# Bias products of the up projection on 32 rows of TensorE, and a new row order in the chunks of w_down

## The chip, the cores and the metric

The kernel runs on one core of a Trainium2 chip. The metric is the device time of one execution in microseconds (us), lower is better. Time before the change: 1526.08 us, the median of three runs (1525.84 to 1527.07).

## The reference

One block of an encoder on 512 frames of width 1024, in float32: a layer norm, a mixer (latent attention with 8 heads and an HGRN2 recurrence with 4 heads, which share one input projection and one output projection `w_o`), a residual with a layer norm, a mixture of 32 experts of which each frame takes four, and a residual with a layer norm. Each expert computes

```
hb  = xb @ w_up[e] + b_up[e]              # 128 slots, 1024 -> 2048
glu, lin = split(hb)                      # 1024 each
act = min(glu, 7) * sigmoid(1.702 * glu) * (clip(lin, -7, 7) + 1)
y   = act @ w_down[e] + b_down[e]         # 1024 -> 1024
```

`b_up` is a table of 32 rows (one for each expert) of 2048 values. The change touches how `b_up[e]` gets into the up projection, how the rows of `w_down[e]` lie in SBUF, and nothing else of the mathematics.

## The kernel before

**Precision.** Every large product is made of three: a float32 value is split into a high part that TensorE takes at its full rate, and the rest, and `mm3` (L408 to L411) adds high times high, high times low and low times high in PSUM.

**The stream of weights.** `Stream` (class at L43) loads w_o in 4 chunks and then, for each expert, w_up in 8 chunks and w_down in 4, each of 1 MB as 128x2048. SP issues the loads (L74) as soon as a raw buffer is free. ACT makes the high part (`w_hi_t`, L87) and DVE the low part (`w_lo_t`, L89); with the low part a raw buffer is free again. Four high and four low buffers stand between the split and TensorE.

**One expert.** `up_begin` (L416) takes four PSUM banks, one for each 512 of the 2048 columns, and puts the bias there first: four bf16 products `bias_mm` (L413 and L414) whose stationary operand is a column of the selector `erow_b`, spread over 128 columns, and whose moving operand is 512 columns of `bias`. `bias` holds the 32 rows of b_up as high, middle and low bf16 parts on partitions 0 to 31, 32 to 63 and 64 to 95, and zeros on the last 32; the selector has a one on the three rows of the expert. Then come 8 chunks of w_up with 12 products each; ACT and DVE make the activation; `act_T` (L446) transposes its 128x512 halves in 128x128 pieces (L451); and 4 chunks of w_down follow, 12 products each, in two banks. Chunk k of w_down holds rows 256k to 256k+255, row p and row 128+p on partition p (`dn_src`, L214), so transposed piece i of the activation is columns 128i to 128i+127. Experts follow one another without a gap, the transposes and routing products of the next expert (L368, small bf16 products on 32 of the columns of TensorE) between the chunks. This stage is in an order written out by hand.

**The mixer.** `run_mixer` is ordered by a scheduler: the program is written as generators that are woven together, and the scheduler then puts each engine's instructions in one order from its own estimates. At the end of the mixer TensorE has the last projections (L938 to L940 with `mw_hi`), whose results ACT and DVE take as `gs` (L1542, L1543); the levels of the recurrence (L1260 and L1271 on TensorE, with a masked copy `hsc`, L1261 and L1273, and a product `QF`, L1283, on DVE between two levels); and the first half of the output projection, `out_part` (L1588), eight groups of 12 products of `w_o` with `cat`. `cat` is the normed attention: `attn_out` makes its high part on ACT (L1408) and its low part on DVE (L1409), four pieces each.

**Preparing the bias.** `prepare_up` (L321, called at L1567, ahead of the loads of the residual rows at L1578 in the program) runs beside the last projections: four loads of b_up (L328) and twelve moves into `bias` (L335) on ACT's queue, three copies of 128x512 on ACT (L331) and two subtractions of 128x512 on DVE (L333). The selector is made once at the start of the program (L147 to L154).

Of the kernel before, what the change touches and what calls it, by code (L numbers as in the profile page):

```python
# [120 lines left out]
class Consts:  # L121
    def __init__(self, nc, pool, tmp):
# [25 lines left out]
        t = tmp.tile([128, NE], F32, name="sel_t")  # L148
        nc.vector.tensor_scalar(self.erow, jp[:, :NE], 0.0, None, op0=ALU.is_equal)
        for r in (1, 2):  # L150
            nc.vector.tensor_scalar(t, jp[:, :NE], -float(r * NE), None, op0=ALU.is_equal)
            nc.vector.tensor_add(self.erow, self.erow, t)
        self.erow_b = pool.tile([128, NE], BF, name="erow_b")
        nc.vector.tensor_copy(self.erow_b, self.erow)  # L154


class Moe:
# [55 lines left out]
    @staticmethod  # L213
    def dn_src(w, k):  # L214
        return [(lambda t: t.rearrange("p (k n) -> p k n", k=2),
                 w[256 * k:256 * (k + 1), :].rearrange("(k p) n -> p k n", p=128))]
# [104 lines left out]
    def prepare_up(self, tmp):  # L321

        nc = self.nc
        nc.gpsimd.memset(self.bias[96:128], 0.0)

        bq = tmp.tile([128, 512], F32, name="prep_b")
        for q in range(4):
            nc.scalar.dma_start(bq[32 * q:32 * q + 32], self.a["b_up"][0][:, 512 * q:512 * q + 512])  # L328
        for r in range(3):
            pt = tmp.tile([128, 512], BF, name=f"prep_p{r}")  # L330
            nc.scalar.copy(pt, bq)  # L331
            if r < 2:
                nc.vector.tensor_sub(bq, bq, pt)  # L333
            for q in range(4):
                nc.scalar.dma_start(self.bias[32 * r:32 * r + 32, 512 * q:512 * q + 512],  # L335
                                    pt[32 * q:32 * q + 32, :])
# [76 lines left out]
    def bias_mm(self, ps, sel, j):  # L413
        self.nc.tensor.matmul(ps, sel, self.bias[:, 512 * j:512 * j + 512], start=True, stop=False)  # L414

    def up_begin(self, sel):  # L416
        ps = [self.ps_up.tile([128, 512], F32, name="ps_up_t") for _ in range(4)]
        for j in range(4):
            self.bias_mm(ps[j], sel, j)
# [26 lines left out]
    def act_T(self, h):  # L446

        nc, ah, al = self.nc, self.ah, self.al
        p = self.ps_tr.tile([128, 4, 128], F32, name="ps_tr", tag="tr")
        for i in range(4):  # L450
            nc.tensor.transpose(p[:, i, :], self.l_bufs[h][:, 128 * i:128 * i + 128], self.c.ident)  # L451
# [122 lines left out]
    def sel_of(self, e):  # L574
        return self.c.erow_b[:, e:e + 1].to_broadcast([128, 128])
# [107 lines left out]
    def overflow(self, out):  # L683
# [3 lines left out]
        with tc.For_i(0, n, 1) as i:  # L687
# [28 lines left out]
            sc = self.xp.tile([128, 1], F32, name="ov_sc")  # L716
# [1017 lines left out]
```

## Time and profile before

| what | value |
|---|---|
| median of 3 runs | 1526.08 us (1525.84 to 1527.07) |
| profiled execution | 1526.0 us |
| its span | 1524.2 us |
| mean granted clock of TensorE | 0.986 of full speed |
| TensorE busy (PE) | 1463.3 us, 96% of the span |
| VectorE busy (DVE) | 1325.1 us, 87% |
| ScalarE busy (ACT) | 1074.7 us, 71% |
| GpSimd busy (POOL) | 263.8 us, 17% |

The profiled execution is 0.08 us under the median and inside the range of the three runs, so its rows may stand for them. The span is 1.8 us shorter than its own time; that rest lies around the span. In all that follows, times are microseconds from the start of the span, and PE is TensorE's products, PEld its loads of the stationary operand. The experts take the stretch from 338 us to about 1495 us; what lies ahead is the layer norm, the mixer and the routing, what lies behind is the last layer norm.

### The profile page before, as it was taken

Reading aid. Unit: us, or ns where it says so; the run is one execution under the profiler, and the core shown is the slowest. Engines: PE = TensorE matmul, PEld = TensorE weight load, DVE = VectorE, ACT = ScalarE, POOL = GpSimd, SP = SyncE. Lnnn points to the kernel's source line nnn. Section 1 sums busy time; section 2 is a strip of 40 time slices with the busy share of each in tenths; the row PEclk is TensorE's granted clock in tenths of the full one; section 3 lists DMA queues with packets and bytes.
Section 4 is the critical chain, followed back from the end, with each engine's and each line's share of the span. In section 5 each row is a group of like instructions: output and inputs, shape, how many; then the busy total and the mean of one; then the engine's idle time right before and its main releaser. Section 6 shows DMA issues by size and latency. Waiting matters only on the chain. (4 is left out here: it accounts for less than half of the span.)

```text
span 1524.2 us, 20021 instructions
## 1 busy us (share of the span) xinstructions
PE 1463.3 (96%) x7366; PEld 1208.1 (79%) x7398; DVE 1325.1 (87%) x1519; ACT 1074.7 (71%) x1149; POOL 263.8 (17%) x249
## 2 busy tenths in 40 slices
PE   7999999979999999999999999999999999999983
PEld 5878998767888888888888888888888888888863
DVE  8867877668999999999999999999999999999975
ACT  4678453347777777777777777777777777777762
POOL 5120414230111111111111111111111111111033
PEclk9999999999999999999999999999999999999997
DMA  5222145367999999999999999999999999999943
GB/s 201 86 81 56 29 147 189 145 212 288 346 366 371 374 358 374 369 377 364 366 376 356 375 361 372 359 378 371 374 359 371 374 368 370 372 366 365 362 152 119
DMA packets 100730, 457.15 MB, mean 300 GB/s; under 512 B 14032, under 2 KB 24697, under 8 KB 67859
## 3 DMA queue, kind: packets, MB, share of 16 engines
q1 hardware_dynamic: 86002, 425.51, 74.4%
q0 software_dynamic: 12672, 29.50, 6.6%
q8 instruction: 60, 0.98, 0.3%
q10 hardware_dynamic: 1952, 0.80, 0.2%
q14 instruction: 44, 0.35, 0.1%
HBM read 447.26 MB, written 24.64 MB: 310 GB/s over the span
## 5 line engine op out<-in xcount | busy, mean ns | idle before, releaser
L89 DVE TENSOR_TENSOR w_lo_t<-w_raw,w_hi_t 128x2048 fp32r<-128x2048 f32 (+1 forms) x391 | 881.3, 2274 | 87.5 <-ACT w_hi_t L87 86.8
L87 ACT CAST w_hi_t<-w_raw 128x2048 fp32r<-128x2048 f32 (+1 forms) x391 | 724.8, 1900 | 1.7 <-PE ps_up_t L411 1.2
L409 PE MATMUL ps_up_t<-w_hi_t,xh 128*128 128x512 f32 x1024 | 420.0, 410 | 0.0
L411 PE MATMUL ps_up_t<-w_hi_t,xl 128*128 128x512 f32 x1024 | 403.4, 394 | 0.0
L410 PE MATMUL ps_up_t<-w_lo_t,xh 128*128 128x512 f32 x1024 | 400.2, 391 | 0.0
L473 POOL DMA_INDIRECT acc_dram<-h,idx x31 | 97.4, 3142 | 955.1 <-ACT h L472 748.4
L411 PEld LDWEIGHTS ps_up_t<-w_hi_t,xl 128*128 128x128 f32 x1024 | 192.7, 188 | 43.6
L409 PEld LDWEIGHTS ps_up_t<-w_hi_t,xh 128*128 128x128 f32 x1024 | 193.2, 189 | 39.7 <-issue 0.8
L410 PEld LDWEIGHTS ps_up_t<-w_lo_t,xh 128*128 128x128 f32 x1024 | 193.4, 189 | 37.4
L411 PE MATMUL ps_dn_t<-w_hi_t,h 128*128 128x512 f32 x512 | 199.8, 390 | 1.1 <-DVE h L455 1.1
L409 PE MATMUL ps_dn_t<-w_hi_t,h 128*128 128x512 f32 x512 | 200.1, 391 | 0.3 <-ACT h L454 0.3
L410 PE MATMUL ps_dn_t<-w_lo_t,h 128*128 128x512 f32 x512 | 199.9, 390 | 0.0
L411 PEld LDWEIGHTS ps_dn_t<-w_hi_t,h 128*128 128x128 f32 x512 | 96.5, 189 | 21.6 <-DVE h L455 1.5
L409 PEld LDWEIGHTS ps_dn_t<-w_hi_t,h 128*128 128x128 f32 x512 | 96.6, 189 | 20.5 <-ACT h L454 0.5
L410 PEld LDWEIGHTS ps_dn_t<-w_lo_t,h 128*128 128x128 f32 x512 | 96.5, 189 | 20.1
L403 ACT CAST xh<-ps_tr 128x512 fp32r<-128x512 f32 x64 | 37.6, 588 | 88.6 <-PE ps_tr L400 88.6
L454 ACT CAST h<-ps_tr 128x512 fp32r<-128x512 f32 x64 | 37.5, 588 | 79.4 <-PE ps_tr L451 79.4
L472 ACT ACTIVATE h<-ps_dn_t,gate_s 128x512 f32<-128x512 f32 x62 | 42.4, 689 | 65.0 <-PE ps_dn_t L411 65.0
L938 PE MATMUL pj<-mw_hi,hT 128*128 128x256 f32 (+1 forms) x192 | 60.2, 314 | 2.8 <-ACT hT L1059 1.7
L939 PE MATMUL pj<-mw_lo,hT 128*128 128x256 f32 (+1 forms) x192 | 58.4, 305 | 1.1 <-DVE mw_lo L866 1.1
L940 PE MATMUL pj<-mw_hi,hT 128*128 128x256 f32 (+1 forms) x192 | 58.2, 303 | 1.3 <-DVE hT L1061 1.3
L433 ACT ACTIVATE act_l<-ps_up_t 128x512 f32<-128x512 f32 x64 | 38.4, 601 | 23.7 <-PE ps_up_t L411 23.7
(363 smaller groups left out, 1803.3 us busy)
## 6 DMA issues: line engine op xcount, KB each, us to landing
w_raw<-in_w_up SPq DMA_DIRECT2D x256, 1024.0 KB
w_raw<-in_w_down SPq DMA_DIRECT2D x128, 1024.0 KB
mw_raw<-in_w_in SPq DMA_DIRECT2D x16, 512.0 KB
w_raw<-in_w_o SPq DMA_DIRECT2D x4, 1024.0 KB
mw_raw<-in_w_in SPq DMA_DIRECT2D x4, 672.0 KB
h_dram<-x POOLq DMA_DIRECT2D x4, 512.0 KB, 3.5
h<-h_dram POOLq DMA_DIRECT2D x4, 512.0 KB, 5.2
rows_dram<-h POOLq DMA_DIRECT2D x4, 512.0 KB, 4.7
```

What stands on the lines that cost most here:

```text
L87: self.nc.scalar.copy(h[:, s], r[:, s])
L89: self.nc.vector.tensor_sub(l[:, s], r[:, s], h[:, s].bitcast(F32))
L403: nc.scalar.copy(xh[:, s, :], p)
L409: mm(ps, xh, wh, start=start, stop=False)
L410: mm(ps, xh, wl, start=False, stop=False)
L411: mm(ps, xl, wh, start=False, stop=stop)
L433: nc.scalar.activation(self.l_bufs[h], ps[2 + h], AF.Copy, bias=1.0)
L472: nc.scalar.mul(y[:, 512 * n:512 * n + 512], ps[n], gate)
L473: nc.gpsimd.indirect_dma_start(out=self.acc[:, :], out_offset=bass.IndirectOffsetOnAxis(ap=idx[:, :1], axis=0), in_=y, in_offset=None, bou ...
L938: mm(ps, xh, wh, start=start, stop=False, skip_group_check=True)
L939: mm(ps, xh, wl, start=False, stop=False, skip_group_check=True)
L940: mm(ps, xl, wh, start=False, stop=stop, skip_group_check=True)
```

## The change

`bias` now uses all 128 partitions in another way. Partitions 32j to 32j+31 belong to the j-th 512 columns of b_up; in them lie 8 experts of three parts each (high, middle, low: partitions 32j+8r+i) and 8 zero rows, and the four groups of 8 experts stand side by side as 4x512 columns. So each of the four bias products of an expert has 32 rows of TensorE instead of 128, on rows 32j to 32j+31, and its selector is the slice of 32 partitions.

`prepare_up` builds that: it clears a 128x2048 tile on POOL, loads b_up into it by twelve DMAs on POOL's queue (three times, one for each part), makes the selector (formerly at the program's start) and a table `later` by some fifteen small instructions on DVE, and then works on whole 128x2048 tiles: ACT copies to bf16, DVE takes off what later parts must not hold, ACT copies again, DVE again, ACT makes `bias`. The twelve moves into `bias` are gone.

`dn_src` lays rows 2p and 2p+1 of a chunk of w_down on partition p, which in the source is one run of 8 KB instead of two of 4 KB; `act_T` takes the activation's columns with a stride of two to match. w_o keeps the old layout by `out_src`. The loop for overflowing slots (cut from the diff) does its bias by 16 products; it is passed through without a turn with these inputs, since the bias products of the trace are four for each of 32 experts.

```diff
--- before.py
+++ after.py
@@ -145,13 +145,7 @@
         nc.gpsimd.iota(self.ecol, pattern=[[1, NE]], base=0, channel_multiplier=0,
                        allow_small_or_imprecise_dtypes=True)
         self.erow = pool.tile([128, NE], F32, name="erow")
-        t = tmp.tile([128, NE], F32, name="sel_t")
-        nc.vector.tensor_scalar(self.erow, jp[:, :NE], 0.0, None, op0=ALU.is_equal)
-        for r in (1, 2):
-            nc.vector.tensor_scalar(t, jp[:, :NE], -float(r * NE), None, op0=ALU.is_equal)
-            nc.vector.tensor_add(self.erow, self.erow, t)
         self.erow_b = pool.tile([128, NE], BF, name="erow_b")
-        nc.vector.tensor_copy(self.erow_b, self.erow)
 
 
 class Moe:
@@ -212,6 +206,11 @@
 
     @staticmethod
     def dn_src(w, k):
+
+        return [(lambda t: t, w[256 * k:256 * (k + 1), :].rearrange("(p two) n -> p (two n)", two=2))]
+
+    @staticmethod
+    def out_src(w, k):
         return [(lambda t: t.rearrange("p (k n) -> p k n", k=2),
                  w[256 * k:256 * (k + 1), :].rearrange("(k p) n -> p k n", p=128))]
 
@@ -320,20 +319,37 @@
 
     def prepare_up(self, tmp):
 
-        nc = self.nc
-        nc.gpsimd.memset(self.bias[96:128], 0.0)
-
-        bq = tmp.tile([128, 512], F32, name="prep_b")
-        for q in range(4):
-            nc.scalar.dma_start(bq[32 * q:32 * q + 32], self.a["b_up"][0][:, 512 * q:512 * q + 512])
+
+        nc, c = self.nc, self.c
+        b = tmp.tile([128, 2048], F32, name="prep_b")
+        nc.gpsimd.memset(b, 0.0)
         for r in range(3):
-            pt = tmp.tile([128, 512], BF, name=f"prep_p{r}")
-            nc.scalar.copy(pt, bq)
+            for j in range(4):
+                p = 32 * j + 8 * r
+                nc.gpsimd.dma_start(b[p:p + 8, :].rearrange("i (g n) -> i g n", g=4),
+                                    self.a["b_up"][0][:, 512 * j:512 * j + 512].rearrange("(g i) n -> i g n", g=4))
+
+        row = tmp.tile([128, 32], F32, name="prep_row")
+        t = tmp.tile([128, 32], F32, name="prep_t")
+        for j in range(4):
+            nc.vector.tensor_scalar(t if j else row, c.slots[:, 0:32], BIG + 32.0 * j, c.pcol,
+                                    op0=ALU.add, op1=ALU.is_equal)
+            if j:
+                nc.vector.tensor_add(row, row, t)
+        later = tmp.tile([128, 2], F32, name="prep_later")
+        for r in range(2):
+            nc.vector.tensor_reduce(later[:, r:r + 1], row[:, 8 * r + 8:24], axis=AX.X, op=ALU.add)
+        nc.vector.tensor_scalar(later, later, -1.0, None, op0=ALU.mult)
+        nc.vector.tensor_add(t[:, 0:8], row[:, 0:8], row[:, 8:16])
+        nc.vector.tensor_add(t[:, 0:8], t[:, 0:8], row[:, 16:24])
+        for x in (c.erow, c.erow_b):
+            nc.vector.tensor_copy(x.rearrange("p (g i) -> p g i", g=4), t[:, None, 0:8].to_broadcast([128, 4, 8]))
+
+        for r in range(3):
+            pt = tmp.tile([128, 2048], BF, name="prep_p") if r < 2 else self.bias
+            nc.scalar.copy(pt, b)
             if r < 2:
-                nc.vector.tensor_sub(bq, bq, pt)
-            for q in range(4):
-                nc.scalar.dma_start(self.bias[32 * r:32 * r + 32, 512 * q:512 * q + 512],
-                                    pt[32 * q:32 * q + 32, :])
+                nc.vector.scalar_tensor_tensor(b, pt, later[:, r:r + 1], b, op0=ALU.mult, op1=ALU.add)
 
     def open(self, ctx, h1, h1_pool):
         tc, nc = self.tc, self.nc
@@ -410,13 +426,13 @@
         mm(ps, xh, wl, start=False, stop=False)
         mm(ps, xl, wh, start=False, stop=stop)
 
-    def bias_mm(self, ps, sel, j):
-        self.nc.tensor.matmul(ps, sel, self.bias[:, 512 * j:512 * j + 512], start=True, stop=False)
-
-    def up_begin(self, sel):
+    def up_begin(self, sels):
+
         ps = [self.ps_up.tile([128, 512], F32, name="ps_up_t") for _ in range(4)]
-        for j in range(4):
-            self.bias_mm(ps[j], sel, j)
+        for i, (sel, g) in enumerate(sels):
+            for j in range(4):
+                p = slice(32 * j, 32 * j + 32)
+                self.nc.tensor.matmul(ps[j], sel[p], self.bias[p, 512 * g:512 * g + 512], start=i == 0, stop=False)
         return ps
 
     def up_chunk(self, ps, x, w, k):
@@ -447,8 +463,10 @@
 
         nc, ah, al = self.nc, self.ah, self.al
         p = self.ps_tr.tile([128, 4, 128], F32, name="ps_tr", tag="tr")
+
+        l = self.l_bufs[h].rearrange("p (k q two) -> p k two q", k=2, two=2)
         for i in range(4):
-            nc.tensor.transpose(p[:, i, :], self.l_bufs[h][:, 128 * i:128 * i + 128], self.c.ident)
+            nc.tensor.transpose(p[:, i, :], l[:, i // 2, i % 2, :], self.c.ident)
         yield
         s = slice(4 * h, 4 * h + 4)
         nc.scalar.copy(ah[:, s, :], p)
@@ -572,7 +590,7 @@
             steps[step[0]](int(step[1]))
 
     def sel_of(self, e):
-        return self.c.erow_b[:, e:e + 1].to_broadcast([128, 128])
+        return [(self.c.erow_b[:, e:e + 1].to_broadcast([128, 128]), e // 8)]
 
     def experts(self, out):
         st = self.st
...
@@ -1639,7 +1657,7 @@
             c = Consts(nc, cp, tmp)
         moe = Moe(tc, ctx, a, c, NE_RUN)
         st = Stream(tc)
-        st.first = [st.add(*Moe.dn_src(a["w_o"][0], k)) for k in range(4)]
+        st.first = [st.add(*Moe.out_src(a["w_o"][0], k)) for k in range(4)]
         moe.add_chunks(st)
         M, S, xp, x, cat, on, out_part, ps, pj, pool = run_mixer(tc, ctx, a, c, moe, st)
         for h in range(HH):
```

Since `run_mixer` is ordered by a scheduler, the new `prepare_up` also moves other instructions. Three places follow; the line numbers of the change are its own, some 18 higher.

First, TensorE (PE) behind the last projections. Here `tr<-ones_f,sq` are the sums for the norm of the attention, `hg` the levels of the recurrence, `tr<-ident,q` transposes and `pj<-w_hi_t,cat` the output projection. Before:

```order
L1583 MATMUL tr<-ones_f,sq 128x1 x4
L1260 MATMUL hg<-q,KG 128x128 x8
L1271 MATMUL hg<-QF,KG 128x64 x4
L938 MATMUL pj<-w_hi_t,cat_3120 128x512 x2
L1271 MATMUL hg<-QF,KG 128x64 x4
L1335 MATMUL tr<-ident,q 128x128 x8
L939 MATMUL pj<-w_lo_t,cat_3120 128x512
L940 MATMUL pj<-w_hi_t,cat_3121 128x512
L938 MATMUL pj<-w_hi_t,cat_3120 128x512
```

With the change:

```order
L1601 MATMUL tr<-ones_f,sq 128x1 x4
L1278 MATMUL hg<-q,KG 128x128 x8
L1289 MATMUL hg<-QF,KG 128x64 x12
L1353 MATMUL tr<-ident,q 128x128
L1289 MATMUL hg<-QF,KG 128x64 x4
L1353 MATMUL tr<-ident,q 128x128 x7
L1289 MATMUL hg<-QF,KG 128x64 x14
L956 MATMUL pj<-w_hi_t,cat_3125 128x512
L957 MATMUL pj<-w_lo_t,cat_3125 128x512
```

The first product with `cat` stood behind 12 products of the recurrence, and now stands behind 38 and 8 transposes.

Second, ACT in the same place: `gs` are the last projections' results, `cat` the attention part of the operand of the output projection, `prep_p` and `bias` the bias rows. Before:

```order
L1542 ACTIVATE gs<-pj 128x256
L328 DMA prep_b<-in_b_up 32x512 x2
L1542 ACTIVATE gs<-pj 128x256
L1408 ACTIVATE cat_3120<-at,cols 128x512 x3
L331 CAST prep_p_3057<-prep_b 128x512
L1542 ACTIVATE gs<-pj 128x256
L335 DMA bias<-prep_p_3057 32x512 x2
L864 CAST mw_hi<-mw_raw 128x256 x4
L1542 ACTIVATE gs<-pj 128x256
L335 DMA bias<-prep_p_3057 32x512 x2
L331 CAST prep_p_3064<-prep_b 128x512
L1408 ACTIVATE cat_3120<-at,cols 128x512
```

With the change:

```order
L1560 ACTIVATE gs<-pj 128x256 x2
L882 CAST mw_hi<-mw_raw 128x256 x4
L1560 ACTIVATE gs<-pj 128x256 x5
L87 CAST w_hi_t<-w_raw 128x2048 x4
L350 CAST prep_p<-prep_b 128x2048 x2
L350 CAST bias<-prep_b 128x2048
L1426 ACTIVATE cat_3125<-at,cols 128x512 x4
L1316 COPY hkg<-hg 128x384 x2
```

The four pieces of `cat` stood between the second and the fifth `gs`; now they stand behind the last `gs`, the four high parts of w_o and the three copies of the bias rows.

Third, DVE behind the last `gs`, where `w_lo_t` are the low parts of w_o and `hsc` and `QF` belong to the recurrence. Before:

```order
L1543 TENSOR_TENSOR gs<-gs,pj 128x256
L1261 COPY_PREDICATED hsc<-masks,hg 128x512 x2
L89 TENSOR_TENSOR w_lo_t<-w_raw,w_hi_t 128x2048 x2
L1273 COPY_PREDICATED hsc<-masks,hg 128x256
L1283 TENSOR_TENSOR QF<-QF,f 128x256
L1273 COPY_PREDICATED hsc<-masks,hg 128x256
L1283 TENSOR_TENSOR QF<-QF,f 128x256
L1607 SCALAR_TENSOR_TENSOR h_0_3109<-pj,rs,h_0_3109 128x512
L89 TENSOR_TENSOR w_lo_t<-w_raw,w_hi_t 128x2048
```

With the change:

```order
L89 TENSOR_TENSOR w_lo_t<-w_raw,w_hi_t 128x2048 x2
L1279 COPY_PREDICATED hsc<-masks,hg 128x512
L89 TENSOR_TENSOR w_lo_t<-w_raw,w_hi_t 128x2048
L1291 COPY_PREDICATED hsc<-masks,hg 128x256
L1301 TENSOR_TENSOR QF<-QF,f 128x256
L89 TENSOR_TENSOR w_lo_t<-w_raw,w_hi_t 128x2048
L1291 COPY_PREDICATED hsc<-masks,hg 128x256
L1301 TENSOR_TENSOR QF<-QF,f 128x256
L352 SCALAR_TENSOR_TENSOR prep_b<-prep_p,prep_later,prep_b 128x2048
L1345 SCALAR_TENSOR_TENSOR q<-hg,h_rs,gs 128x128 x4
L1291 COPY_PREDICATED hsc<-masks,hg 128x128x2
L352 SCALAR_TENSOR_TENSOR prep_b<-prep_p,prep_later,prep_b 128x2048
```

Two instructions of 128x2048 on `prep_b` now stand among the steps of the recurrence; the next `QF` is the row behind the last one shown, behind the second of them. One `hsc` of 128x512 stands ahead of the first row.

## Rows read from the trace of the kernel before

**Rows 1.** Busy time by stretch, expert stage: columns as in its heading row.

```profile
core 0: us, PE busy (x) PEld busy (x) DVE busy (x) ACT busy (x) POOL busy (x), PEclk, DMA share, GB/s
...
455.00:490.00 35.00, 34.93 (x162) 28.45 (x163) 32.06 (x23) 27.12 (x22) 4.47 (x2) 1.00 0.99 371
```

**Rows 2.** Waits, 420 to 1440 us: total, times, longest; then the queue of SP, whole span.

```profile
DVE w_lo_t L89 <- ACT w_hi_t L87: 76.2, 137, 1.1
...
PEld L414 <- issue: 7.6, 29, 0.3
...
SPq L74 <- DVE w_lo_t L89: 819.3, 307, 25.7
```

**Rows 3.** Timeline of PE around one set of bias products: start, duration, group.

```profile
654.67 0.39 PE L411 MATMUL ps_dn_t<-w_hi_t,h 128*128 128x512 f32 x1
655.13 0.81 PE L414 MATMUL ps_up_t<-bias,erow_b 128*128 128x512 bf16 x3
...
656.01 0.39 PE L410 MATMUL ps_up_t<-w_lo_t,xh 128*128 128x512 f32 x1
656.24 0.40 PE L411 MATMUL ps_up_t<-w_hi_t,xl 128*128 128x512 f32 x1
```

**Rows 4.** The bias products by source line: duration min/median/max, first and last start.

```profile
L414 PE MATMUL ps_up_t<-bias,erow_b x98: 376/379/634, 338.7 to 1439.9; 128*128 128x512 bf16 x98
```

**Rows 5.** Timeline of PE and PEld around the small products of line 368.

```profile
391.31 0.39 PE L411 MATMUL ps_up_t<-w_hi_t,xl 128*128 128x512 f32 x1
...
391.63 0.27 PE L368 MATMUL ps_tr<-vals,oh 128*32 128x5 bf16 x16
...
392.16 0.39 PE L410 MATMUL ps_up_t<-w_lo_t,xh 128*128 128x512 f32 x1
```

**Rows 6.** Timeline of PE, first expert.

```profile
338.73 1.49 PE L414 MATMUL ps_up_t<-bias,erow_b 128*128 128x512 bf16 x3
```

**Rows 7.** The transposes of the activation by source line.

```profile
L451 PEld LDWEIGHTS ps_tr<-ident,act_l x256: 138/140/146, 373.0 to 1482.1; 128*128 128x128 f32 x128
```

**Rows 8.** Timeline of PE from the end of the projections.

```profile
242.40 0.95 PE L1583 MATMUL tr<-ones_f,sq 128*128 128x1 f32 x8
243.21 2.03 PE L1260 MATMUL hg<-q,KG 128*128 128x128 f32 x16
245.18 1.10 PE L1271 MATMUL hg<-QF,KG 128*128 128x64 f32 x8
246.10 0.72 PE L938 MATMUL pj<-w_hi_t,cat 128*128 128x512 f32 x2
```

**Rows 9.** Busy time by stretch, from the end of the projections to LN1.

```profile
242.40:286.30 43.90, 43.60 (x288) 38.81 (x286) 34.45 (x64) 13.35 (x26) 20.39 (x21) 1.00 0.41 145
286.30:305.00 18.70, 16.54 (x75) 13.02 (x74) 13.03 (x25) 7.77 (x11) 2.20 (x4) 1.00 0.79 298
```

**Rows 10.** Timeline of ACT and of DVE, then groups of DVE with mean ns.

```profile
223.98 1.94 ACT L1408 ACTIVATE cat<-at,cols 128x512 fp32r<-128x512 f32 x3
...
242.88 3.69 ACT L87 CAST w_hi_t<-w_raw 128x2048 fp32r<-128x2048 f32 x2
...
244.38 0.74 DVE L1261 COPY_PREDICATED hsc<-masks,hg 128x512 f32<-128x512 uint8 x1 [0.31 <-PE hg L1260]
...
L89 DVE TENSOR_TENSOR w_lo_t<-w_raw,w_hi_t 128x2048 fp32r<-128x2048 f32 x27 | 61.8, 2310 | 5.8 <-ACT w_hi_t L87 5.8
...
L1283 DVE TENSOR_TENSOR QF<-QF,hE 128x256 f32<-128x256 f32 x12 | 7.5, 624 | 0.0
L1273 DVE COPY_PREDICATED hsc<-masks,hg 128x256 f32<-128x256 uint8 x14 | 7.3, 522 | 2.5 <-PE hg L1271 1.9
```

**Rows 11.** Waits of PE under the last projections, 218 to 243 us.

```profile
PE pj L938 <- DVE gs L1543: 1.1, 2, 0.7
```

**Rows 12.** Busy time of PE and granted clock in the 3.4 us windows of the page.

```profile
34.67:38.08 3.41, 1.74 (x11) 1.00 0.00 0
38.08:41.49 3.41, 3.41 (x14) 0.50 0.01 2
```

More of the change, by code (lines that the diff above doesn't have):

```diff
@@ L715, in overflow @@
             nc.vector.tensor_mul(et, self.c.erow, em)
-            sc = self.xp.tile([128, 1], F32, name="ov_sc")
-            nc.vector.tensor_reduce(sc, et, axis=AX.X, op=ALU.add)
-            sel_t = self.xp.tile([128, 1], BF, name="ov_sel")
+            sc = self.xp.tile([128, 4], F32, name="ov_sc")
+            nc.vector.tensor_reduce(sc, et.rearrange("p (g i) -> p g i", g=4), axis=AX.X, op=ALU.add)
+            sel_t = self.xp.tile([128, 4], BF, name="ov_sel")
             nc.vector.tensor_copy(sel_t, sc)
-            sel = sel_t.to_broadcast([128, 128])
+            sel = [(sel_t[:, g:g + 1].to_broadcast([128, 128]), g) for g in range(4)]
             wu = a["w_up"][0][bass.ds(e, 1)].rearrange("o k n -> (o k) n")
```

## Prediction

> **What bounds the kernel now.** I began with the busy times by stretch, since the whole span hides stages with different limits. In the expert stage TensorE works 34.93 of 35 us at full clock, DVE 32.06 and ACT 27.12 [rows 1]: TensorE bounds it, and what an expert's products cost is what an expert costs. The DMA share of 0.99 looks like a second bound, so I read the waits next. Of an engine that waits for a DMA there is no row in that view; the longest wait is DVE for ACT, and the queue of SP waits 307 times for DVE to free a raw buffer [rows 2]. The loads are held back by the splits, which keep pace with TensorE; they do not hold anything. The mixer's end came third, because the order of the instructions changes there: from the last projection to the end of the first half of the output projection TensorE is busy 43.60 of 43.90 us [rows 9]. Any hole made there is lost in full; behind it, up to LN1, it idles 2.16 us.
>
> **The bias products.** Four per expert, 98 of 128 of them recorded, 379 ns long each [rows 4], but pipelined. The price is the distance of their neighbours: L411 starts at 654.67, the second product behind the block, L410, at 656.01 [rows 3]. That is 1.34 us, where two steps of 0.23 (656.01 to 656.24) would be 0.46. So the block costs 0.88, and the three records agree: 0.81 less one length of 0.38, over two, is 0.215 a product, 0.86 for four.
>
> On 32 rows each, the four can run side by side, so the block is one product of 0.215 and little more for the other three starts. But TensorE goes from whole-array products to tiles and back. The nearest row is L368, 16 products on 32 columns each: L411 to the second product behind takes 391.31 to 392.16, 0.85 us [rows 5], so 0.39 more than two steps. Their own work is between nothing and the 0.27 of their record; I take 0.10, hence 0.29 for both switches (0.12 to 0.39). Block: 0.215 + 0.02 + 0.29 = 0.52 us, **0.36 saved** per expert, 11.2 over 31 experts (bounds 8 to 17 by the switch; 20 if it costs nothing). The first expert's three records take 1.49 [rows 6], 0.43 a product, the half clock; it saves about 0.9. Together **-12.1 us**.
>
> The Trainium skill bears on this from both sides. "TensorEngine Tiling (Array Packing)", Key Properties, says that a change of the tiling mode drains TensorE; the extra 0.39 of [rows 5] agrees that the passage is not free, and gives it the price. "TensorE: Matmul & The Clock Gate", Part 3, gives 3.07 times for four row tiles with 512 columns; by that the block would be an estimated 0.88 / 3.07 = 0.29 us and the saving 0.59, 18 us over 31 experts. I stay with the row, since that figure need not hold a passage from and to whole-array products for every four.
>
> **The rows of w_down.** The bytes stay, the runs get longer. As no engine waits for these loads, I cost a faster load at nothing; the cover is the held-back queue [rows 2], and if it were gone TensorE would wait for ACT's split. The transposes now read with a stride of two. Their weight load takes 140 ns, 256 of them [rows 7]; no row shows a strided one of float32. Between no loss and twice the time lie 0 and 256 x 0.14 = 36 us. I take 0: the number and the size of the elements read stay the same, only their distance grows.
>
> **The preparation.** Gone are four loads, twelve moves, three copies and two subtractions of 128x512, all under the projections, where TensorE lost 1.1 us to `gs` [rows 11], perhaps because ACT and DVE had them to do. I give this back: **-1.1** (0 to -1.1). The memset and the twelve DMAs on POOL precede POOL's loads of the residual rows, which wait for TensorE's last projection anyway; nothing. The fifteen small DVE instructions lie under the projections, whose bound is TensorE; nothing.
>
> The cost is the order. Before, `cat` was made from 223.98 on [rows 10], and the output projection began at 246.10 [rows 8]. Now three engines chain:
> - ACT: four high parts from 242.88 at 1.85 each [rows 10] end at 250.3; the first copy of 128x2048, taken as one such split, ends at 252.2.
> - DVE, from 244.38: two `hsc` of 0.74, four low parts of 2.31, and two pairs `hsc` and `QF` of 0.52 + 0.62 [rows 10]: 1.48 + 9.24 + 2.28 = 13.0, so 257.4. The first long instruction on `prep_b`, taken as a low part, ends at 259.7.
> - ACT's second copy: 261.6. DVE's second long one: 263.9. ACT's `bias`: 265.8, the first `cat` (1.94 / 3 = 0.65 [rows 10]) 266.5.
> - TensorE is in order, and the last levels of the recurrence stand ahead of `cat`. They need four `QF` behind 263.9, with two `hsc` between that wait for TensorE: 263.9 + 4 x 0.62 + 3 x 0.52 + half a level of 0.5 is **268.4** for the first product of the output projection.
>
> From 242.40 to 268.4 is 26.0 us. TensorE's work in it: 0.8 for the sums and 2.0 for the first level, start to start, and 30 products, of which four (8 records) take about 1.0, with the transposes put at another 1.0 [rows 8]: 0.8 + 2.0 + 7.5 + 1.0 = 11.3. So 14.7 idle instead of 0.3: **+14.4** (12.5, if `cat` alone decides at 266.5; 16.4, if every step on the way waits a tenth longer). Nothing makes up for it, because that work would have fitted between the products of the output projection, where TensorE was full [rows 9]. The 2.16 idle behind may shrink: **-1.0** (0 to -2.2).
>
> A hole also touches the clock. At 34.67 TensorE was busy 1.74 in a window, and the next was granted 0.50 [rows 12], 1.2 instead of 2.4 GHz. My hole has 11.3 in 26.0, some 1.5 per such window. Output projection at half clock for one window of 3.41 us costs **+1.7** (0 to 3.4).
>
> Sum for the mixer: 14.4 - 1.1 - 1.0 + 1.7 = +14.0 (9 to 19). With -12.1 for the products it is +1.9 on the profiled execution's 1526.0: **1527.9 us**; the median is 0.08 above that execution, which changes nothing. A measurement of this kernel tells about 0.2%, 3.05 us, from no change; this stays within it.
>
> **Rivals.**
> - *Faster: the products cost no passage.* [Rows 5] mix the passage with a wait for small work, so the 0.29 could be largely the 16 products. Then the block is 0.28, 0.60 saved x 31 = 18.6, with 1.3 at the first expert 19.9: 1526.0 + 14.0 - 19.9 = 1520.1. The rule of Part 3 above would give nearly the same. The same time comes from a chain before `cat` that is 6 us shorter. Against it speaks that the step into L368 and the step out of it are both long.
> - *Slower: the chain ACT, DVE, ACT, DVE, ACT ahead of `cat`.* Its place is 250 to 268 us; it decides alone once the mixer loses over 12.1 + 3.05 = 15.2. With the high end of the hole (16.4), two windows at half clock (3.4), nothing given back and nothing won under the projections it is +19.8: 1526.0 + 19.8 - 12.1 = 1533.7; with half of these surplus terms, 1531. For it speaks that all engines wait for each other there; against it, that my terms already hold most of it.
> - *The change doesn't do what it says.* If the four products run one after another, the block is 0.86 + 0.29 = 1.15, 0.27 worse than now, +8.4: 1526.0 + 14.0 + 8.4 = 1548. If the strided transposes are at their bad end it would be +36, over 1560. For this speaks no row; the L368 products, on four tiles, pass in 0.27 for 16.
>
> **How the numbers follow.** Forecast 0.42, its own range 1523 to 1532 by the ends of hole and switch; faster rival 0.30 (1520, down to 1516); slower rival 0.21 (1531, up to 1534); failed promise 0.07 (over 1540). The forecast's case lies within 0.2% (1523.0 to 1529.1) in seven of ten, and else is mostly slower. Faster: 0.30 x 0.9 + 0.42 x 0.08, about 0.31. Same: 0.42 x 0.7 + 0.03 + 0.21 x 0.2, about 0.36. Slower: the rest, 0.33. The range 1517 to 1533 leaves out the failed promise, and the outer ends of the two other rivals.
>
> **What would show it.** The first output product at 266 to 269 us instead of 246, with ACT's three long copies ahead of `cat`, and a fall of PEclk about 250 to 270; the first bias products of expert 0 some 14 us later than 338.7; four bias records that start together and L411 to L410 around them in 0.98 (0.46 + 0.52) instead of 1.34 us; PEld of L451 still at 140 ns; no wait on a DMA between experts. I am wrong if `cat` comes early, if the four records start 0.2 apart, if the passage is under 0.1 or over 0.4 us, or if the experts' transposes lengthen.

## The result, and the profile after

The changed kernel takes 1537.99 us (median of four runs, 1537.42 to 1539.83), the kernel before 1525.96 in the same session (four runs, 1523.94 to 1527.07): **0.78% slower**, ratio 1.0078 with an interval of 1.0064 to 1.0092. The profiled execution took 1537.99 us, its span is 1536.2 us, 12.0 longer than that of before.

First the page of the changed kernel: TensorE's busy time, the granted clock in the 40 slices, and the DMA packets.

```profile
PE 1470.0 (96%) x7396; PEld 1217.0 (79%) x7398; DVE 1331.0 (87%) x1527; ACT 1078.2 (70%) x1149; POOL 266.8 (17%) x261
...
PEclk8999997999999999999999999999999999999997
...
DMA packets 84153, 457.28 MB, mean 298 GB/s; under 512 B 14159, under 2 KB 24440, under 8 KB 34898
```

PE is busy 6.7 us longer than before, not shorter, although the products that the change makes cheaper are cheaper: the seventh slice stands at 0.7 of the clock in the row PEclk, with nines on both sides. That slice is 230 to 269 us. The packets fell by a sixth, from 100730 to 84153, by the longer runs of w_down, and the time gained nothing by it.

The difference of 12.0 splits at two marks, the first and the last set of bias products. The first starts at 357.3 instead of 338.7: the mixer and the routing take **18.6 us longer**. From the first set to that of the last expert it is 1092.4 us (357.32 to 1449.75) where it was 1100.8 (338.73 to 1439.51): **8.4 shorter**. Behind it, 1.7 longer. 18.6 - 8.4 + 1.7 = 11.9.

The mixer's end, TensorE's timeline (start, duration, group, idle before), to be held against [rows 8]:

```profile
243.28 0.95 PE L1601 MATMUL tr<-ones_f,sq 128*128 128x1 f32 x8
...
265.04 6.21 PE L1289 MATMUL hg<-QF,KG 128*128 128x64 f32 x28 [0.72 <-DVE QF L1301]
271.00 0.77 PE L956 MATMUL pj<-w_hi_t,cat 128*128 128x512 f32 x1
271.57 0.63 PE L957 MATMUL pj<-w_lo_t,cat 128*128 128x512 f32 x1
```

The last projection ends at 243.3 (before 242.4), and the first product of the output projection starts at 271.00 (before 246.10). The chain ahead of it, ACT's and then DVE's timeline in the same stretch, against [rows 10]:

```profile
243.76 7.29 ACT L87 CAST w_hi_t<-w_raw 128x2048 fp32r<-128x2048 f32 x4
250.95 1.90 ACT L350 CAST prep_p<-prep_b 128x2048 bf16<-128x2048 f32 x1
259.73 1.90 ACT L350 CAST prep_p<-prep_b 128x2048 bf16<-128x2048 f32 x1 [6.88 <-DVE prep_b L352]
264.04 1.90 ACT L350 CAST bias<-prep_b 128x2048 bf16<-128x2048 f32 x1 [2.42 <-DVE prep_b L352]
265.97 2.56 ACT L1426 ACTIVATE cat<-at,cols 128x512 fp32r<-128x512 f32 x4
...
257.35 2.34 DVE L352 SCALAR_TENSOR_TENSOR prep_b<-prep_p,prep_later,prep_b 128x2048 f32<-128x2048 bf16 x1
...
261.66 2.35 DVE L352 SCALAR_TENSOR_TENSOR prep_b<-prep_p,prep_later,prep_b 128x2048 f32<-128x2048 bf16 x1 [0.29 <-ACT prep_p L350]
```

The steps come as the prediction had them: ACT's first long copy ends at 252.9, DVE's first at 259.7, ACT's second at 261.6, DVE's second at 264.0, ACT's third at 265.9, then `cat`. And the granted clock (columns: stretch, length and PE's busy time, clock, DMA share, GB/s):

```profile
246.60:250.00 3.40, 0.61 (x6) 0.80 0.94 363
...
263.70:267.10 3.40, 2.67 (x13) 0.50 0.00 0
...
270.50:273.90 3.40, 3.40 (x11) 0.50 0.00 0
273.90:277.30 3.40, 3.40 (x13) 0.70 0.00 0
```

In the first of these stretches TensorE was busy 0.61 of 3.4 us, and its granted clock went from 1.00 to 0.50, 1.2 GHz (0.80 is the mean of that stretch); it stayed there not for one such stretch but until about 276, over all of the recurrence's last levels (28 records in 6.2 us, where [rows 8] has 8 in 1.1) and the first 5 us of the output projection, whose products stand 0.43 apart (271.57 to 272.00 and so on) instead of 0.23.

Under the projections, where the prediction hoped for a small gain, one wait of 2.8 us has come, DVE's rows and then PE's:

```profile
225.15 0.25 DVE L346 CAST erow_b<-prep_t 128x32 bf16<-128x32 f32 x1
225.44 0.42 DVE L1561 TENSOR_TENSOR gs<-gs,pj 128x256 f32<-128x256 f32 x1
...
225.91 0.38 PE L956 MATMUL pj<-mw_hi,hT 128*128 128x256 f32 x1 [2.79 <-DVE gs L1561]
```

`gs` stood behind the small instructions that make the selector and the table `later`, and TensorE waited for `gs`. Before, it lost 1.1 us here [rows 11].

Now the experts. Around one set of bias products, against [rows 3]:

```profile
671.93 0.39 PE L427 MATMUL ps_dn_t<-w_hi_t,h 128*128 128x512 f32 x1
672.25 0.40 PE L435 MATMUL ps_up_t<-bias,erow_b 32*128 32x512 bf16 x4
672.58 0.51 PE L425 MATMUL ps_up_t<-w_hi_t,xh 128*128 128x512 f32 x1
672.92 0.40 PE L426 MATMUL ps_up_t<-w_lo_t,xh 128*128 128x512 f32 x1
```

From L427 to the second product behind the set it is 0.99 us, where it was 1.34. The four appear as one row of 0.40, as long as one of them alone; the two sources, bias products and the weight loads of the transposes, against [rows 4, 7]:

```profile
L435 PE MATMUL ps_up_t<-bias,erow_b x128: 372/385/605, 357.3 to 1449.8; 32*128 32x512 bf16 x128
...
L469 PEld LDWEIGHTS ps_tr<-ident,act_l x256: 194/206/212, 392.3 to 1493.9; 128*128 128x128 f32 x128
```

The strided weight load takes 206 ns, where the contiguous one took 140.

### The profile page after: what moved, and what is told of

The parts are those of the page before. It is cut to its first block, busy times and chain, and to the rows that moved or that the text cites. A ratio compares the mean times of both kernels' runs of the same rounds, so it can differ in the third digit from the quotient of the medians.

```text
span 1536.2 us, 20060 instructions
## 1 busy us (share of the span) xinstructions
PE 1470.0 (96%) x7396; PEld 1217.0 (79%) x7398; DVE 1331.0 (87%) x1527; ACT 1078.2 (70%) x1149; POOL 266.8 (17%) x261
## 2 busy tenths in 40 slices
DMA packets 84153, 457.28 MB, mean 298 GB/s; under 512 B 14159, under 2 KB 24440, under 8 KB 34898
## 5 line engine op out<-in xcount | busy, mean ns | idle before, releaser
L427 PE MATMUL ps_up_t<-w_hi_t,xl 128*128 128x512 f32 x1024 | 403.1, 394 | 0.0
L427 PEld LDWEIGHTS ps_up_t<-w_hi_t,xl 128*128 128x128 f32 x1024 | 193.1, 189 | 43.4
L427 PE MATMUL ps_dn_t<-w_hi_t,h 128*128 128x512 f32 x512 | 200.3, 391 | 0.4 <-DVE h L473 0.4
L427 PEld LDWEIGHTS ps_dn_t<-w_hi_t,h 128*128 128x128 f32 x512 | 96.7, 189 | 21.0 <-DVE h L473 0.8
```

The lines of the kernel that those rows point to most:

```text
L427: mm(ps, xl, wh, start=False, stop=stop)
```

## The experiments

All ratios are to the kernel before in the same session. "First product" is that of the output projection, "first bias" the first set of bias products; before they are at 246.1 and 338.7, in the change at 271.0 and 357.3. "Period" is the mean distance of the bias sets of the third and the last expert, over 29: 35.645 us before, 35.337 in the change.

**Taking the two halves of the change apart.** The new rows of w_down alone, put into the kernel before:

```diff
-            nc.tensor.transpose(p[:, i, :], self.l_bufs[h][:, 128 * i:128 * i + 128], self.c.ident)
+            nc.tensor.transpose(p[:, i, :], l[:, i // 2, i % 2, :], self.c.ident)
```

(with `dn_src` and `out_src` as in the change.)

> The kernel before with only the new row order of w_down (and the transposes with a stride of two). Theory A (the strided weight load of the transposes is dearer, and no engine gains from longer runs): weight loads of the transposes at 206 ns instead of 140, 0.06 to 0.07 us more per expert, 1527 to 1529 us. Theory B (longer runs help the loads): under 1525 us. Theory C (hidden): 1526 us.

Measured 1527.51 us, ratio 1.0002 (0.9992 to 1.0012), first bias 338.7, period 35.655; the strided loads take 207 ns. Theory C: dearer by half, and hidden, but for 0.010 us per expert. The longer runs bring nothing either. The reverse, the change without its new rows:

> The change without its new row order of w_down: the bias products and their preparation alone. Theory A (strided transposes cost 2 us): 1535 to 1536.5 us, expert period 0.35 us under that of the kernel before. Theory C (hidden): 1538 us, period 0.29 us under.

Measured 1536.60 us, ratio 1.0066 (1.0046 to 1.0086), first bias 358.9, period 35.302. The bias products gain 0.343 us per expert by themselves; beside them the strided transposes cost 0.035. But for that 1 us in all, the loss is in the bias half, ahead of the first expert.

**Whether the four products really run side by side.** All four on the same rows:

```diff
-                p = slice(32 * j, 32 * j + 32)
+                p = slice(0, 32)
```

> The change, but all four bias products of an expert use rows 0 to 31 of TensorE, so that three of the four quarters of the bias are those of the first 512 columns. Theory A (the gain is that the four run side by side, and a fixed passage is paid beside it): the four start 0.21 to 0.22 us apart, the block is 0.65 us longer than in the change, and the time is 1555 to 1560 us. Theory B (the gain is that 32 rows are cheaper than 128, also one after another): the block grows by less than 0.3 us and the time stays under 1548 us.

Measured once, 1559.51 us, period 35.939. PE's timeline around one set:

```profile
717.86 0.39 PE L427 MATMUL ps_dn_t<-w_hi_t,h 128*128 128x512 f32 x1
718.18 1.03 PE L435 MATMUL ps_up_t<-bias,erow_b 32*128 32x512 bf16 x4
...
719.48 0.39 PE L426 MATMUL ps_up_t<-w_lo_t,xh 128*128 128x512 f32 x1
```

Now the set's row is 1.03 us long, and 1.62 us lie between L427 and the second product behind, 0.63 more than in the change. Theory A: 32 rows are no cheaper than 128 by themselves, the gain is that four run at once, and a passage of some 0.31 us (0.99 - 0.46 - 0.22) is paid beside it. With four products one after another the same sum gives 0.28 (1.62 - 0.46 - 4 x 0.22).

**Why cat came late.** The order of the change looked like a choice. The tiles of the preparation are 12.3 KB of each partition instead of 5.1; if they reach into the place that `cat` gets, it is no choice. Two kernels: the change with the preparation in halves of 1024 columns (6.4 KB), and the kernel before with 4 KB left empty ahead of its small tiles.

```diff
+        for q in range(2):
+            b = tmp.tile([128, 1024], F32, name="prep_b")
...
-            pt = tmp.tile([128, 2048], BF, name="prep_p") if r < 2 else self.bias
+                pt = (tmp.tile([128, 1024], BF, name="prep_p") if r < 2
+                      else self.bias[:, 1024 * q:1024 * q + 1024])
```

> The change, with the preparation of the bias rows done in two halves of 1024 columns one after the other, so that its tiles take about 6.4 KB of each partition instead of 12.3 KB and no longer reach into the bytes of cat. Theory A (memory: cat had to wait in the changed kernel because the preparation's tiles lay in its bytes): cat is made under the projections again, the first product of the output projection stands within 3 us of the 246.1 of the kernel before, the first bias product within 3 us of 338.7, and the time is 1517 to 1522 us, faster than both kernels. Theory B (work: the long copies on ACT and DVE hold the stage wherever their tiles lie): the first bias product comes at 350 or later and the time is 1530 or more.

Measured 1537.83 us, ratio 1.0067 (1.0049 to 1.0084). `cat` is early and the first product starts at 246.2, as theory A had it; the first bias still comes at 357.1, as theory B had it. So shared bytes did make `cat` late, but an early `cat` wins nothing here. The timelines of ACT, PE and DVE tell where the time went instead; the last row is the last level in the kernel before:

```profile
221.33 1.95 ACT L1428 ACTIVATE cat<-at,cols 128x512 fp32r<-128x512 f32 x3 [1.26 <-POOL sq L1423]
...
276.49 1.89 PE L1291 MATMUL hg<-QF,KG 128*128 128x64 f32 x16
278.86 2.00 PE L1291 MATMUL hg<-QF,KG 128*128 128x64 f32 x16 [0.48 <-DVE hsc L1293]
282.76 3.53 PE L1291 MATMUL hg<-QF,KG 128*128 128x64 f32 x16 [1.89 <-DVE QF L1303]
286.92 7.06 PE L1291 MATMUL hg<-QF,KG 128*128 128x64 f32 x32 [0.63 <-DVE QF L1303]
...
280.40 1.42 DVE L354 SCALAR_TENSOR_TENSOR prep_b<-prep_p,prep_later,prep_b 128x1024 f32<-128x1024 bf16 x1
...
272.05 1.00 PE L1271 MATMUL hg<-QF,KG 128*128 128x64 f32 x8
```

Now it is the recurrence that comes late. In the kernel before its levels stand between the products of the output projection, and the last one ends at 273.0. Here the new order has none of them from 258.4 to 276.5; then they follow without other products between them, with the long DVE steps of the preparation's second half among them (the first at 280.40; TensorE waits 2.5 us for `QF`), from 282.8 to 293.8 at a granted clock of 0.50. The last one ends at 294.0. No run shows why the order put them off.

```diff
+        nc.gpsimd.memset(tmp.tile([128, 1024], F32, name="prep_pad")[:, 0:4], 0.0)
         bq = tmp.tile([128, 512], F32, name="prep_b")
```

> The kernel before with 4 KB left empty ahead of the preparation's small tiles, so that they reach into the bytes of cat; nothing else. Theory A (sharing bytes alone holds cat back): all four pieces of cat stand behind the last short copy of the preparation, at 238 to 243 us instead of 224 to 234; since that is still ahead of 246, the time rises by less than 3 us, to 1526 to 1529. Theory B (it is the length of the work that puts cat late): cat stays at 224 to 234.

Measured once, 1525.37 us, with the kernel before at 1526.23 (1525.44 to 1528.32) in that session. ACT's timeline:

```profile
234.86 0.62 ACT L332 CAST prep_p<-prep_b 128x512 bf16<-128x512 f32 x1 [0.25 <-issue]
...
239.59 2.56 ACT L1409 ACTIVATE cat<-at,cols 128x512 fp32r<-128x512 f32 x4 [0.40 <-DMA bias<-prep_p]
```

`cat` waits for the last moves of the preparation, at 239.59 instead of 223.98: theory A on the mechanism. And it costs nothing, since the short preparation is through before 246. Shared bytes alone are no loss. That they are one when the work ahead is a long chain is how the trace of the change reads; no run takes that chain out and leaves the rest.

**What the clock cost.** The change with two batches of 16 products without use on `prep_p`, which run in the hole:

```diff
             nc.scalar.copy(pt, b)
+            if r < 2:
+                p = pj.tile([128, 512], F32, name="warm", tag="s")
+                for k in range(16):
+                    nc.tensor.matmul(p, c.ones, pt[:, 512 * (k % 4):512 * (k % 4) + 512], start=True, stop=True)
```

> The change with two batches of 16 products without use in the hole ahead of the output projection, each behind one of ACT's long copies of the preparation. If the half clock there costs 4.4 us of the loss (1.7 within the hole, 2.7 in the first products of the output projection), the granted clock is back at 1.0 when the output projection begins, and the time is 3 to 5 us under that of the change, 1533 to 1535. If the clock costs nothing on this path: 1538, or more by the products added.

PE's busy time and clock by stretch in this run:

```profile
260.40:263.80 3.40, 3.40 (x30) 1.00 0.20 84
...
267.20:270.60 3.40, 3.40 (x27) 1.00 0.00 0
```

The full clock is back from 260 on, the first product starts at 268.8 and the first bias at 353.3, 4.0 earlier than in the change (0.4 of it ahead of the end of the projections): the size that was expected of the clock. The fillers also hold up the chain, ACT makes `bias` 1.3 us later, so it isn't the clock alone that differs. The time is less clear: four runs from 1532.76 (the profiled one) to 1540.76, median 1536.35, ratio 1.0072 (1.0056 to 1.0087). The profile shows the 4 us in one execution; as a gain of the kernel they aren't settled.

**Whether it is the size of the work or its place.** First the short preparation of the kernel before (copies and subtractions of 128x512) with 48 small moves into the new layout, half of them on ACT's queue and half on POOL's:

```diff
+            for j in range(4):
+                for g in range(4):
+                    (nc.scalar, nc.gpsimd)[g % 2].dma_start(
+                        self.bias[32 * j + 8 * r:32 * j + 8 * r + 8, 512 * g:512 * g + 512],
+                        pt[32 * j + 8 * g:32 * j + 8 * g + 8, :])
```

> The bias products on 32 rows, but prepared as in the kernel before: tiles of 128x512, three short copies and two short subtractions, then 48 small moves into the new places; the selector is made at the program's start, and w_down keeps its old row order. Theory A' (what the change lost lies in the large preparation, by its place in the order or its long copies; the products themselves gain 0.34 us each): first bias product within 3 us of 338.7, 0.34 us less per expert, 1513 to 1518 us, faster than both kernels. Rival (the passage to tiles costs elsewhere, or the moves hold the stage): 1521 us or more.

Measured 1530.59 us, ratio 1.0028 (1.0017 to 1.0040), period 35.302, first bias 352.2. The rival. ACT's queue, and PE:

```profile
246.49 0.38 ACT L1554 ACTIVATE gs<-pj 128x256 f32<-128x256 f32 x1 [1.78 <-DMA bias<-prep_p]
246.51 3.32 ACTq L344 DMA_DIRECT2D bias<-prep_p  x5
249.87 3.70 ACT L87 CAST w_hi_t<-w_raw 128x2048 fp32r<-128x2048 f32 x2 [3.00 <-DMA bias<-prep_p]
...
251.82 1.22 PE L950 MATMUL pj<-w_hi_t,cat 128*128 128x512 f32 x2 [6.87 <-ACT w_hi_t L87]
```

The last `gs` and the high parts of w_o stand behind 24 moves at 0.66 us each; `w_hi_t` starts at 249.87 instead of 242.88, TensorE waits 6.87 us for it, and its granted clock is 0.50 from 252 to 260. With the new rows of w_down as well:

> As the run with the small preparation, and with the new row order of w_down and strided transposes. If the strided weight loads cost as in the change against the run without them (0.035 us per expert): 1 to 2 us above the run with the small preparation, 1515 to 1519 us. If they are hidden: the same time within 1 us.

Measured 1531.94 us, ratio 1.0033 (1.0022 to 1.0043), period 35.337: again 0.035 us per expert for the strided transposes, 1 us in all.

Then the long preparation of the change, unaltered, but called behind the first layer norm, far from the output projection:

```diff
     lns.close()
+    with ExitStack() as t9:
+        moe.prepare_up(pool(t9, "mx_btmp", side="left"))
```

> The bias products and the long preparation of the change, with the preparation written some 170 us earlier in the program (behind the first layer norm, ahead of the projections of the recurrence), and the old row order of w_down. The work is the same, to the instruction; the place is another, and the order at the end of the mixer is that of the kernel before. Theory A' (the loss of the change is the place of the preparation: cat and the levels of the recurrence behind it): first product of the output projection within 3 us of 246.1, first bias product within 3 us of 338.7, 0.34 us less per expert, 1513 to 1518 us, faster than both kernels. Theory B (the long copies cost their time on ACT and DVE wherever they are): what the end of the mixer wins is lost earlier, first bias product at 346 or later, 1522 us or more.

> The whole change, new row order of w_down included, with only the preparation written earlier, as in the run above. Theory A': 0 to 2 us above the run above (the strided transposes), 1513 to 1519 us, faster than both kernels. Theory B: 1523 us or more.

Measured 1542.20 us (1.0107, 1.0090 to 1.0124) and 1543.72 us (1.0113, 1.0096 to 1.0130): a miss. At the mixer's end all is as before, from the last projection to the first product 3.7 us; but the last projection ends at 266.7 instead of 242.4. The chain found another stage whose softmax and evictions share ACT and DVE with it. PE's waits from 60 to 246 us (total, times, longest), where the kernel before has 1.1 us at most in a row:

```profile
PE s L957 <- ACT a_p L1388: 5.1, 1, 5.1
PE pj L957 <- DVE Vp L963: 4.5, 3, 2.1
PE pj L957 <- ACT f L1549: 3.1, 1, 3.1
```

Two places, then, where the queues had no room. A third is behind the first half of the output projection in the program: what is written there should come last in the scheduler's choice, and fill what the others leave. Once with the short preparation and all moves on SP, which has nothing to issue there, once with the long one in halves, as in the first experiment on memory; both with the old rows of w_down.

```diff
         drain(g)
+    with ExitStack() as t9:
+        moe.prepare_up(pool(t9, "mx_btmp", side="left"))
     hgs.close()
```

> The bias products on 32 rows, with the short preparation (three copies and two subtractions of 128x512), written behind the output projection's first half in the program, and all its loads and 48 moves on SP's queue, which has nothing to issue between 219 and 248 us in the kernel before; old row order of w_down. Theory C (what costs is that steps which wait for one another, or issue many moves, stand in the queues of ACT and POOL ahead of work that the output projection needs; the products' gain is untouched by it): the output projection begins within 3 us of 246.1, first bias product within 4 us of 338.7, 1513 to 1519 us, faster than both kernels. Rival (any preparation of this layout in the mixer costs about what it cost so far, by contention or by the clock): 1526 us or more.

> The bias products on 32 rows with the long preparation in two halves, written behind the output projection's first half in the program, old row order of w_down. The order puts cat under the projections and the first half of the long steps (three copies of 1.04 us) on ACT behind two high parts of w_o. Theory C: the output projection begins within 3 us of 246.1 and has no hole over 6 us in its first half, first bias product within 6 us of 338.7, 1514 to 1523 us. Rival (the work of the long steps itself holds the stage): first bias product at 350 or later, 1528 us or more.

Measured **1517.29 us, ratio 0.9941 (0.9927 to 0.9954)**, and 1519.97 us, ratio 0.9956 (0.9941 to 0.9972): both faster than the kernel before and than the change, theory C. The first product starts at 246.8 and 249.3, the first bias comes at 342.5 and 342.0, the period is 35.302 in both. Of the short one, SP, ACT and PE:

```profile
235.56 16.05 SPq L344 DMA_DIRECT2D bias<-prep_p  x23
253.22 0.84 SPq L74 DMA_DIRECT2D w_raw<-in_w_up  x2
254.12 19.19 SPq L344 DMA_DIRECT2D bias<-prep_p  x25
...
239.17 0.62 ACT L339 CAST prep_p<-prep_b 128x512 bf16<-128x512 f32 x1 [0.76 <-DVE prep_b L341]
240.40 0.39 ACT L1554 ACTIVATE gs<-pj 128x256 f32<-128x256 f32 x1 [0.61 <-PE pj L952]
...
243.56 7.30 ACT L87 CAST w_hi_t<-w_raw 128x2048 fp32r<-128x2048 f32 x4
...
246.77 0.71 PE L950 MATMUL pj<-w_hi_t,cat 128*128 128x512 f32 x2
...
L429 PE MATMUL ps_up_t<-bias,erow_b x128: 371/385/605, 342.5 to 1432.2; 32*128 32x512 bf16 x128
```

ACT's copies fall between two `gs` for which it waits anyway, and the high parts start at 243.56. The moves go out on SP; they put off its loads of w_up, which begin at 253.22 instead of 248.21 and go on behind 273, and TensorE waits for none of them. This run differs from the one with the short preparation above in two things, place and queue, and doesn't part them. Of the long one, the busy times (columns as in [rows 9]) of the stretches in which the output projection's first half runs:

```profile
243.00:266.00 23.00, 22.72 (x159) 20.57 (x158) 18.61 (x28) 10.88 (x9) 13.62 (x14) 1.00 0.49 183
266.00:286.00 20.00, 20.00 (x137) 18.13 (x136) 14.91 (x26) 3.29 (x15) 11.26 (x18) 1.00 0.36 124
```

TensorE is full. The two kernels with halves hold the same long steps of the same sizes and differ in the place in the program (and in the rows of w_down, worth 1 us): 1537.8 against 1520.0. So it is not the work, it is its place: what the order puts behind it in the queues.

## Why the prediction was wrong

- **The bias products** were right: 0.53 us for the set (0.99 - 0.46) against 0.52, 0.343 us saved against 0.36. The passage to tiles and back was priced by [rows 5] at 0.29, and 0.31 was found. That it came so close is partly luck: those rows are of products on 32 columns, not on 32 rows, and the 0.10 taken off for their own work was a choice. The rule of the Trainium skill ("TensorEngine Tiling (Array Packing)", Key Properties) that a change of tiling mode drains TensorE agrees with the 0.31 us, in that the passage is not free. The 3.07 times that the Trainium skill gives ("TensorE: Matmul & The Clock Gate", Part 3) isn't what a set between whole-array products gets: 0.88 / 0.53 is 1.7.
- **What the experts gained** was mis-sized, -8.4 for -12.1. Of the 3.7, 1.0 is the strided transposes, costed at nothing although the prediction named a longer weight load as a sign of being wrong; 0.5 is the bias sets; 0.4 is the last expert's own set, which lies behind the mark. The other 1.8 lie in the first two experts, which together take 0.6 us longer, where 1.3 less was forecast; the distance from the second expert's set to the third's is 41.6 for 40.6. The rows of w_down don't explain that: the run with the fillers has them and 40.6, the short preparation has 41.5 with them and without. The granted clock goes along with it. In the first expert it stands at 0.50 for 3.9 us from the first set on, where the kernel before has 3.1, and between the second set and the third for 6.8 us where it has 3.4. So it is in all 14 kernels: eight have 3.4 us there and a distance of 40.4 to 41.0, the six others 6.8 us and 41.5 to 41.6. A stretch of it in the change, then in the kernel before:

```profile
385.20:391.90 6.70, 5.33 (x12) 0.50 0.84 340
...
369.20:372.50 3.30, 3.30 (x9) 0.50 0.96 376
```

No run shows why the half clock lasts longer in some kernels.

- **The chain ahead of cat** was right step by step, to 0.2 us from DVE's first long step on, up to `bias` at 265.9. The first product came 1.7 us later than its sum, counted from the last projection (27.7 for 26.0): the chain was 0.9 shorter, but the levels behind DVE's second long step, put at 4.5 us, took 7.1 (263.9 to 271.0), all of it at half clock.
- **The clock** is the step that failed most plainly: it was priced at half clock for 3.41 us, the length of the stretches in [rows 12] (the slices of the page are 38.1 us long), +1.7 with 3.4 as its end, and for the output projection alone. An estimate from the rows is 4.1: 1.8 in the levels (28 records in 5.96 us, where the first experiment on memory has 16 in 2.37 at full clock), and 2.3 in the output projection (12 steps in 5.11 us, where 0.31 and eleven of 0.23 make 2.8), not 2.7 as the run with the fillers was expected to save there. That run agrees with the sum: from the last projection to the first bias it takes 110.4 us, the change 114.0. The prediction had the fall from [rows 12], but not that the half clock also slows the last part of the very chain that ends the hole, nor that it would last until about 276.
- **Under the projections** the sign was wrong: the wait of 1.1 us, which was to go, became one of 2.8, by the fifteen small DVE instructions that were costed at nothing. Their cover was said to be TensorE's own work, and `gs` stood behind them on DVE: a wait on DVE's queue, not on its time. The last projection ended 0.9 later and not 1.7, since this execution was some 0.6 us ahead up to there. Such a lead is no part of the change: the same wait of 0.5 us comes at 190.0 to 192.3 in kernels that are alike up to that point.
- **Behind the last expert's set** 1.7 us came that no step named. The run without the new rows has 84.9 us there, the kernel before 84.7, the change 86.4, and the first experiment on memory 87.0; it differs between kernels that do the same work there. The time at a clock of 0.50 behind the set is 25.4, 25.3, 28.0 and 28.5 us in these four, but the order doesn't hold over all runs (with the four products on the same rows it is 23.6, for 85.1 us), so its cause stays open.

Added up against the prediction's terms: 2.0 up to the last projection (-1.1 became +0.9), 1.7 from there to the first output product, 0.9 from there to the first bias set (6.3 won back, where the prediction's terms make 7.2; 0.6 of it the clock), 3.7 in the experts and 1.7 behind are 10.0 of the 10.1 us between 1527.9 and 1538.0. Of these, the 1.8 in the first two experts go with the granted clock, and only the 1.7 behind the last have no known cause. The rival that was slower, by this very chain, had the right place; its price ended at 1533.7, because its ends were those of terms that all erred to one side.

The words that the order had moved `cat` were true and not yet a cause. The tiles had grown into its bytes, and two runs show that this decides where `cat` stands. The loss is decided by what the order puts behind the preparation: of five other ways to prepare the same rows three lost as well, each at another place.

## What to carry to other kernels

Work that runs once may cost more than a saving in every pass of the loop, if its steps wait for one another and stand in the in-order queues of engines that feed the bound one: price what is queued behind each step, DMA issues included, not its busy time. Put such work last in a scheduler's program order, and its moves on a queue that is idle, before shortening it; the two faster runs did the first, and one of them both. When tiles grow, look whose bytes they take: the scheduler must then put their work ahead of the next owner's.

## What the runs showed of the hardware

- Four products on 32 rows each take as long as one (0.40 us in a row for 0.385 alone), 1.03 on the same 32 rows, and each set between whole-array products pays about 0.3 us more (0.31 side by side, 0.28 on the same rows).
- A weight load of 128x128 in float32 with a stride of two elements takes 206 ns instead of 140, and in the stream of products only 0.010 to 0.035 us per expert (eight loads) of it are seen.
- Loads in runs of 8 KB instead of 4 KB, with a sixth fewer packets in all, changed nothing in a stage where the loads wait for free buffers: 1.0002 (0.9992 to 1.0012).
- The granted clock fell from 1.00 to 0.50 (1.2 GHz) within 3.4 us in which PE was busy 0.61, and still stood there from 267.1 to 273.9, where PE was busy all the time.
- Kernels that do the same work, but for the bias set, between the second expert's and the third's set stand there at 0.50 for 3.4 or for 6.8 us, and take 40.4 to 41.0 or 41.5 to 41.6 us (eight and six kernels, one profile each).
